# One transformer-like layer in fp32: the rotary step moved from GpSimd to VectorE, and three changes to the order of the output products

## The chip, the core and the metric

The kernel runs on one core of a Trainium2 chip. The metric is the device time of one execution in microseconds (us), shown as the median of three runs. The core has five engines that each follow their own list of instructions: TensorE (PE, with its weight loads as PEld), VectorE (DVE), ScalarE (ACT), GpSimd (POOL) and SyncE (SP), which issues most of the transfers (DMA). They wait for each other through semaphores; each executes its list in order.

## What is computed

One layer over 2,048 prompt tokens and 32 sample tokens, model width 1,024, everything in fp32. Cut to what matters here:

```python
h = rmsnorm(x, ln_g)
q, k, v, gate_a, b_gate, c_gate, u_in, gate_c, merge_a, merge_c = split(h @ w_in)
q = rope(rmsnorm(q.reshape(b, t, 8, 64), q_norm_g), pos)     # per head of 64
k = rope(rmsnorm(k.reshape(b, t, 2, 64), k_norm_g), pos)
attn = banded attention of q, k, v in chunks of 64, with sinks
y_a = (attn * silu(gate_a)) @ w_attn_out                     # "yA", 512 -> 1024
y_c = (b_gate * conv3(c_gate * u_in) * silu(gate_c)) @ w_conv_out   # "yB"
r = x + (sigmoid(merge_a) * y_a + sigmoid(merge_c) * y_c) @ w_o     # "o"
out = r + sigmoid(r @ w_ple_gate) * (p @ w_ple_proj)         # "pg" and "pp"
```

The rotary step of one head x with halves x1, x2 is `[x1*cos - x2*sin, x2*cos + x1*sin]`. Since the norm's factor is one number for a head and token, it may be applied ahead of the rotation or behind it.

## The kernel before

**Products.** Every operand of a matmul is split into a high and a low part (`hi` by an ACT cast, `lo` by a DVE subtraction), and each product is three matmuls. So each piece of weights, 128x512 numbers, costs an ACT cast and a DVE subtraction after its load. All of this keeps PE at 98% of the span.

**Two stages.** The first stage (to 855 us of the span) makes h @ w_in and writes q, k, v, the gates and the conv rows to DRAM. The change touches only the second stage, which starts there: attention in 17 tiles of 128 tokens (one of 32), woven by single matmuls into the output products. Tokens stand in four blocks b of 512 (the last has 544). A unit of products is named by kind, block and column group: `yB0_3`, `pp2_1`, `yA0_4`, `o0_2`, `pg0_7`. Blocks 1 and 2 share Strassen-like products for o and pg (`b50_n_p` and `b58_n_p`: matrix 50 is w_o, 58 is w_ple_gate, p one of seven products, n a column group), and block 3 makes them by quadrants (`s50..`, `s58..`).

**What sets the order.** `plan` (line 272) lists the units by hand. While the program is written, a planner in the kernel keeps a clock `now` with fixed prices for each engine and writes instructions in the order of that clock; helpers are generators that hand back their needs (`yield {"ps": 2}` asks for two PSUM banks) and go on when these are free. So most instructions of the second stage have the line of the recording helper, L135, and are told apart by tiles. Nothing is reordered at run time: an instruction that waits holds up those behind it on its engine.

**The rotary step** (`attention`, from line 1310). For a tile, PE transposes q and k, v into PSUM (`pq`, `pkv`). ACT squares them into `qn`, DVE sums the squares (`ss`), adds EPS, and GpSimd takes the power -1/2 and makes `ab`, cos and sin times the norm weights. DVE then multiplies q and k from PSUM by `ss` into `qn` (128x512 and 128x128). The rest is GpSimd's: the products `tt` with cos and sin (128x256 for k, 128x1024 for q), and the sums `kr` (two of 128x128) and `qr` (two of 128x256). PE transposes `kr` and `qr` (`pk`, `pqt`), ACT and DVE split them (`KH`/`KL`, `qs`), and the scores `S` follow. GpSimd also issues the transfers that add a DRAM row to a row in SBUF (`ta<-z_t`, `tk<-z_t`, `c<-in_xT`).

**Other names that are used below.** `ta`, `tk`: rows of yA with their gate; `m_l`, `ac_l`, `p_l`, `xb_l`, `r_l`, `rq_l`: low parts of rows for the next product; `pf`: rows of p as loaded; `w<-wr`: the split of a weight piece; `at<-O,ga`: a chunk's output times its gate; `nm<-S`, `se`: the softmax's maximum and sum; `ptl`, `pth`: the transposed probabilities.

**Weights and rows.** `next_loads` issues a raw piece when one of 8 raw buffers is free and it is under 8 pieces beyond the split ones (five); `split_w` splits pieces in order. `load_p` loads rows of p; block 3's are loaded again for each pair of `pp` units (four times).

## Time and profile before

| | us |
|---|---|
| median of 3 runs | 1529.82 |
| lowest, highest run | 1529.79, 1532.02 |
| the profiled execution | 1532.24 |
| its span, first to last instruction | 1530.5 |
| PE busy | 1501.7 (98%) |
| DVE busy | 1206.2 (79%) |
| ACT busy | 836.3 (55%) |
| POOL busy | 468.3 (31%) |
| the second stage, from yB's first product to the last matmul's end | 855.8 to 1525.5 |

A row of the trace gives the start (us from the span's start), the duration, engine, line, operation, `out<-in` by tiles, and in brackets how long the engine was idle ahead of it and who ended that. A matmul's bar is longer than the time to the next one, since matmuls overlap; so waits are read from PE's idle brackets and from the difference of a window's length and PE's busy time.

### The profile page before, as it was taken

How to read it: one execution, taken by the hardware profiler on the slowest of the kernel's cores; microseconds unless marked ns; L12 is line 12 of the kernel's file. 1: busy time of each engine (PE TensorE's matmuls, PEld its weight loads, DVE VectorE, ACT ScalarE, POOL GpSimd, SP SyncE). 2: the span in 40 equal slices, each digit the busy share in tenths (PEclk: the TensorE clock that was granted, in tenths of full speed). 3: DMA queues.
4: the chain of work that ended last, by engine and by line, in shares of the span. 5: the costliest groups of instructions: out<-in, count | busy, mean ns of one | idle time of the engine just before them, and what ended most of it. 6: DMA issues, size and time to landing. Idle time of an engine off the chain costs nothing.

```text
span 1530.5 us, 27077 instructions
## 1 busy us (share of the span) xinstructions
PE 1501.7 (98%) x9025; PEld 1333.8 (87%) x9025; DVE 1206.2 (79%) x2208; ACT 836.3 (55%) x1966; POOL 468.3 (31%) x634
## 2 busy tenths in 40 slices
PE   9999999999999999999999999989999999999898
PEld 7878888888889999999999889978887877888898
DVE  7896887875589766898955787898967789785886
ACT  8453354344467544434554566767775475653575
POOL 2133332332212232333232245462433334112112
PEclk9999999999999999999999999999999999999999
DMA  9479886798778845343555786685678838879998
GB/s 341 154 280 342 308 293 232 276 342 279 241 266 268 307 141 196 117 132 115 184 191 185 266 302 216 217 245 188 201 193 217 220 93 205 223 209 319 289 311 253
DMA packets 207292, 357.94 MB, mean 234 GB/s; under 512 B 24624, under 2 KB 61552, under 8 KB 207152
## 3 DMA queue, kind: packets, MB, share of 16 engines
q1 hardware_dynamic: 165216, 252.40, 50.9%
q0 software_dynamic: 32288, 85.99, 19.3%
q10 hardware_dynamic: 9648, 17.83, 3.1%
q8 instruction: 71, 1.16, 0.3%
q14 instruction: 69, 0.57, 0.1%
HBM read 238.77 MB, written 117.46 MB: 233 GB/s over the span
## 4 chain that ended last, share of the span: by engine, by line
PE 41%; DVE 5%; DMA 4%; issue 2%; ACT 1%; SPq 0%; POOL 0%; DVEq 0%; ACTq 0%
PE b L135 7%; PE yB L135 6%; PE yA L135 3%; PE o L135 3%; PE pg L135 3%; PE O L135 2%; DMA pf<-in_pT 2%; PE S L135 2%; PE s58a L135 1%; PE la L722 1%; DMA wr<-in_wu 1%; PE a L589 1%; PE a L586 1%; PE a L584 1%; PE s50a L135 1%
## 5 line engine op out<-in xcount | busy, mean ns | idle before, releaser
L586 PE MATMUL a<-x_l,w 128*128 128x264 f32 (+1 forms) x744 | 228.2, 319 | 0.0
L584 PE MATMUL a<-x_h,w 128*128 128x264 f32 (+1 forms) x744 | 227.3, 320 | 0.4 <-DVE s L790 0.4
L589 PE MATMUL a<-x_h,w 128*128 128x264 f32 (+1 forms) x744 | 201.4, 320 | 0.0
L135 ACT CAST w<-wr 128x512 fp32r<-128x512 f32 x204 | 123.7, 621 | 87.2 <-PE b L135 30.9
L135 DVE TENSOR_TENSOR w<-wr,w 128x512 fp32r<-128x512 f32 x204 | 154.0, 765 | 18.3 <-ACT w L135 16.8
L206 ACT CAST w<-wr 128x512 fp32r<-128x512 f32 (+1 forms) x180 | 110.1, 618 | 105.8 <-PE c L589 30.7
L207 DVE TENSOR_TENSOR w<-wr,w 128x512 fp32r<-128x512 f32 (+1 forms) x180 | 131.0, 738 | 36.9 <-ACT w L206 35.6
L584 PEld LDWEIGHTS a<-x_h,w 128*128 128x128 f32 x744 | 139.8, 188 | 11.0 <-DVE s L790 0.6
L586 PEld LDWEIGHTS a<-x_l,w 128*128 128x128 f32 x744 | 140.1, 188 | 10.3
L135 PE MATMUL b<-xb_h,w 128*128 128x512 f32 x448 | 142.7, 395 | 1.8 <-ACT w L135 1.1
L589 PEld LDWEIGHTS a<-x_h,w 128*128 128x128 f32 x744 | 125.2, 188 | 10.8
L722 PE MATMUL la<-x_h,w 128*128 128x264 f32 x516 | 111.9, 285 | 1.7 <-ACT w L206 1.2
L584 PE MATMUL c<-x_h,w 128*128 128x512 f32 (+1 forms) x336 | 110.5, 339 | 0.0
L586 PE MATMUL c<-x_l,w 128*128 128x512 f32 (+1 forms) x336 | 110.4, 338 | 0.0
L135 PEld LDWEIGHTS b<-xb_h,w 128*128 128x128 f32 x448 | 83.4, 188 | 21.0 <-DVE w L135 1.6
L206 ACT CAST w<-a 128x512 fp32r<-128x512 f32 x82 | 49.7, 620 | 94.3 <-DVE a L342 30.9
L589 PE MATMUL c<-x_h,w 128*128 128x512 f32 (+1 forms) x336 | 99.9, 338 | 0.0
L783 DVE SCALAR_TENSOR_TENSOR u<-u,c 128x264 f32<-128x264 f32 (+1 forms) x125 | 59.4, 507 | 42.7 <-ACT u L778 28.4
L778 ACT COPY u<-a 128x264 f32<-128x264 f32 (+1 forms) x114 | 47.4, 437 | 79.7 <-PE a L589 75.5
L135 PE MATMUL yA<-ac_h,w 128*128 128x512 f32 (+1 forms) x320 | 89.0, 358 | 1.6 <-DVE ta L135 1.0
L722 PEld LDWEIGHTS la<-x_h,w 128*128 128x128 f32 x516 | 87.0, 189 | 2.4 <-ACT w L206 1.4
L135 PE MATMUL b<-xb_l,w 128*128 128x512 f32 x224 | 88.3, 394 | 0.0
(535 smaller groups left out, 4310.2 us busy)
## 6 DMA issues: line engine op xcount, KB each, us to landing
wr<-in_wu SPq DMA_DIRECT2D x213, 256.0 KB, 4.2
a<-in_wu SPq DMA_DIRECT2D x116, 256.0 KB, 5.1
wr<-ws SPq DMA_DIRECT2D x74, 256.0 KB, 3.5
wr<-qs SPq DMA_DIRECT2D x64, 256.0 KB, 4.6
ws<-a POOLq DMA_DIRECT2D x63, 256.0 KB, 3.8
qs<-a POOLq DMA_DIRECT2D x24, 256.0 KB, 5.7
tb<-z_t SPq DMA_DIRECT2D x24, 256.0 KB, 4.9
z_t<-tb SPq DMA_DIRECT2D x24, 256.0 KB, 4.3
```

The costliest lines, as they stand in the source:

```text
L135: return f(**kw)
L206: nc.scalar.copy(out=hi, in_=src)
L207: nc.vector.tensor_tensor(out=lo, in0=src, in1=hi.bitcast(F32), op=sub)
L584: nc.tensor.matmul(out=ps[:, :cn], lhsT=w[:, 0, k], rhs=x[0][:, c0:c0 + cn], start=first and k == 0, stop=False, skip_group_check=True)
L586: nc.tensor.matmul(out=ps[:, :cn], lhsT=w[:, 0, k], rhs=x[1][:, c0:c0 + cn], start=False, stop=False, skip_group_check=True)
L589: nc.tensor.matmul(out=ps[:, :cn], lhsT=w[:, 1, k], rhs=x[0][:, c0:c0 + cn], start=False, stop=k == 3, skip_group_check=True)
L722: nc.tensor.matmul(out=ps[:, :m], lhsT=w[:, a, k], rhs=r[:, cols], start=q in "ABG" and j == 0 and e == 0, stop=j == 1 and e == 2, skip_gr ...
L778: nc.scalar.copy(out=t[:, c0:c0 + cn], in_=ps[:, :cn])
L783: nc.vector.scalar_tensor_tensor(out=t[:, c0:c0 + cn], in0=t[:, c0:c0 + cn], scalar=-1.0, in1=ps[:, :cn], op0=mul, op1=sub)
```

## The change

Five edits, all in the second stage.

1. The rotary step. `ab` is made first, on GpSimd. DVE multiplies q and k straight from PSUM with `ab` into `tt`, without the norm's factor; ACT squares into a tile `sq` whose 65th column holds EPS, so that the sum includes it; DVE adds the halves into `kn` and `qr`; and at the end DVE multiplies by `ss` into `kr` and `qr`. GpSimd keeps the power and `ab`.
2. `plan`'s start: yB of blocks 0 and 1 first, then yB of 2 and 3 with pp of block 2 between; pp of block 3, units 2 to 5, among and behind yA of block 0 instead of near the end.
3. `plan`'s end: block 3's yA stands among pg's products from the 18th of 28 on (before: from the 22nd, with the last one behind all), and two pg products come behind the last yA.
4. Weights: raw pieces are loaded up to eleven ahead of the piece in use, and a split buffer is given back 0.5 us (of the planner's clock) after its last use.
5. Rows of p for block 3: three loads instead of four.

```diff
-    plan = [("yB", b + e, n) for b in (0, 2) for n in range(8) for e in range(2)]
-    plan += [("pp", 2, n) for n in range(8)] + [("yA", 0, n) for n in range(8)] + [("pp", 3, 0), ("pp", 3, 1)]
+    plan = [("yB", e, n) for n in range(8) for e in range(2)]
+    for n in range(8):
+        plan += [("yB", 2, n), ("yB", 3, n), ("pp", 2, n)]
+    plan += [("pp", 3, 0), ("pp", 3, 1)] + [("yA", 0, n) for n in range(5)]
+    plan += [("pp", 3, 2), ("yA", 0, 5), ("pp", 3, 3), ("yA", 0, 6), ("yA", 0, 7), ("pp", 3, 4), ("pp", 3, 5)]
...
-    plan += tail[:21]
-    for e, part in enumerate(tail[21:]):
-        plan += [part, ("yA", 3, NA[3][e])]
-    plan += [("pp", 3, 2), ("pp", 3, 3), ("yA", 3, NA[3][7]), ("pp", 3, 4), ("pp", 3, 5)]
+    plan += tail[:17]
+    late = [("yA", 3, n) for n in NA[3]]
+    for e, part in enumerate(tail[17:27]):
+        plan += [part] + ([late.pop(0)] if e not in (2, 9) else [])
+    plan.append(tail[27])
...
+        ab = sm.tile([P, 2, 2, 64], F32, tag="ab", name=f"ab{b}_{i}", bufs=1)
+        eG.tensor_tensor(out=ab[:n], in0=cs[:n].unsqueeze(1).to_broadcast([n, 2, 2, 64]),
+                        in1=qkg_sb[:n].unsqueeze(2).to_broadcast([n, 2, 2, 64]), op=mul)
...
+        for q, (h0, hn, src) in enumerate(q3):
+            eV.tensor_tensor(out=tt[:n, h0:h0 + hn], in0=src[:n].unsqueeze(2).to_broadcast([n, hn, 2, 64]),
+                            in1=ab[:n, q].unsqueeze(1).to_broadcast([n, hn, 2, 64]), op=mul)
...
-        eV.tensor_reduce(out=ss[:n], in_=qn[:n], axis=AX.X, op=add)
-        eV.tensor_scalar(out=ss[:n], in0=ss[:n], scalar1=EPS, scalar2=None, op0=add)
+        eV.tensor_reduce(out=ss[:n], in_=sq[:n], axis=AX.X, op=add)
...
+        for d in (0, 32):
+            for o, h in ((kn, slice(8, 10)), (qr, slice(0, 8))):
+                eV.tensor_tensor(out=o[:n, :, d:d + 32], in0=tt[:n, h, 0, d:d + 32], in1=tt[:n, h, 1, 32 - d:64 - d], op=add)
...
-        for h0, hn, src in q3[::-1]:
-            eV.tensor_tensor(out=qn[:n, h0:h0 + hn], in0=src[:n], op=mul,
-                            in1=ss[:n, h0:h0 + hn].unsqueeze(2).to_broadcast([n, hn, 64]))
...
-        for h0, hn, q in ((8, 2, 1), (0, 8, 0)):
-            eG.tensor_tensor(out=tt[:n, h0:h0 + hn],
...
-        for d in (0, 32):
-            eG.tensor_tensor(out=qr[:n, :, d:d + 32], in0=tt[:n, 0:8, 0, d:d + 32],
-                            in1=tt[:n, 0:8, 1, 32 - d:64 - d], op=add)
+        eV.tensor_tensor(out=kr[:n], in0=kn[:n].unsqueeze(2).to_broadcast([n, 2, 2, 64]),
+                        in1=ss[:n, 8:10].unsqueeze(2).unsqueeze(3).to_broadcast([n, 2, 2, 64]), op=mul)
+        eV.tensor_tensor(out=qr[:n], in0=qr[:n], in1=ss[:n, 0:8].unsqueeze(2).to_broadcast([n, 8, 64]), op=mul)
...
-        while n_raw[0] < len(worder) and busy["Y"] < now[0] + 0.5 and (
-                n_raw[0] < RAWS or raw_free[n_raw[0] - RAWS] <= now[0]) and n_raw[0] < len(made) + RAWS:
+        while n_load[0] < min(len(worder), used[0] + LOOK) and busy["Y"] < now[0] + 0.5:
...
-    for i, at_ in enumerate(("yB2_5", "yA0_2", f"yA3_{NA[3][2]}", f"yA3_{NA[3][4]}", f"s{UO}_2_2")):
+    for i, at_ in enumerate(("yB0_7", "yB2_5", "yA0_3", f"s{UO}_2_2")):
```

How the rows of an engine move is seen best at two places. The first is the tile `2_0` (the first of block 2), whose rotary step stands among the last yA of block 0. GpSimd's list there before, from the tile's power to the end of its sums:

```order
L135 TENSOR_TENSOR ss2_0_12274<-ss2_0_12274,nhalf_70 128x10
L135 TENSOR_TENSOR ab2_0_12316<-cs2_0_12091,cst_69 128x256
L135 DMA ta0_4_12121<-z_t1_4_112 128x512
L135 TENSOR_TENSOR tt2_0_12383<-qn2_0_12261,ab2_0_12316 128x256
L135 DMA ta0_5_12166<-z_t1_5_113 128x512
L135 TENSOR_TENSOR tt2_0_12383<-qn2_0_12261,ab2_0_12316 128x1024
L135 TENSOR_TENSOR kr2_0_12385<-tt2_0_12383 128x4x32 x2
L135 TENSOR_TENSOR qr2_0_12384<-tt2_0_12383 128x8x32 x2
```

and in the changed kernel:

```order
L135 DMA ta0_3_12143<-z_t1_3_111 128x512
L135 DMA ta0_4_12170<-z_t1_4_112 128x512
L135 TENSOR_TENSOR ab2_0_12403<-cs2_0_12183,cst_69 128x256
L135 TENSOR_TENSOR ss2_0_12453<-ss2_0_12453,nhalf_70 128x10
L135 DMA ta0_5_12284<-z_t1_5_113 128x512
L135 COPY KH_10068<-KH_10068 128x2x128
```

The six products and sums are gone from GpSimd. On DVE before, the same tile has the two multiplications by `ss` and, behind them, what DVE does while GpSimd works on the tile:

```order
L135 TENSOR_TENSOR qn2_0_12261<-pkv2_0_12253,ss2_0_12274 128x128
L135 TENSOR_TENSOR qn2_0_12261<-pq2_0_12248,ss2_0_12274 128x512
L135 SCALAR_TENSOR_TENSOR ta0_5_12166<-ta0_5_12166,yA0_5_0_12285 128x512
L135 TENSOR_TENSOR KL_10069<-pk1_3_12328,KH_10068 128x2x128
L135 SCALAR_TENSOR_TENSOR ta0_6_12222<-ta0_6_12222,yA0_6_0_12347 128x512
L135 TENSOR_TENSOR qs1_3_12342<-pqt1_3_12331,qs1_3_12342 64x2x256
L135 SCALAR_TENSOR_TENSOR m0_3_l_12367<-ta0_3_12069,m0_3_h_12366 128x512
L135 TENSOR_TENSOR ta0_6_12222<-ta0_6_12222,tc0_6_12224 128x512
L135 TENSOR_TENSOR qs1_3_12342<-pqt1_3_12331,qs1_3_12342 64x2x256
```

and in the changed kernel, the tile's end:

```order
L135 TENSOR_TENSOR kn2_0_12415<-tt2_0_12413 128x2x32
L135 TENSOR_TENSOR qr2_0_12414<-tt2_0_12413 128x8x32
L135 TENSOR_TENSOR kn2_0_12415<-tt2_0_12413 128x2x32
L135 TENSOR_TENSOR qr2_0_12414<-tt2_0_12413 128x8x32
L135 SCALAR_TENSOR_TENSOR ta0_6_12367<-ta0_6_12367,yA0_6_0_12505 128x512
L135 RECIPROCAL se_14_12526<-se_14_12526 128x4
L135 TENSOR_TENSOR w390_12547<-wr390_12145,w390_12547 128x512
L135 TENSOR_TENSOR at1_2_12112<-O_12_12554,ga1_2_12110 128x4x64
L135 TENSOR_TENSOR kr2_0_12416<-kn2_0_12415,ss2_0_12453 128x256
L135 TENSOR_TENSOR qr2_0_12414<-qr2_0_12414,ss2_0_12453 128x512
```

DVE now holds four sums and two scalings of the tile in its own list, and two products from PSUM ahead of them. The second place is ACT's list near the end, where block 3's yA and the last pg products are made. Before, the rows of p (`p2`, `p3`) are split there, among the weight pieces:

```order
L135 ACTIVATE rq1_50_0_h_16659<-ta3_4_16455 128x544
L135 CAST p2_0_h_16676<-pf2_0_16586 128x544
L135 ACTIVATE c21_58_0_6_16089<-c21_58_0_6_16089 128x512
L135 CAST p2_1_h_16684<-pf2_1_16597 128x544
L135 ACTIVATE rq2_50_0_h_16661<-rta50_0_16669 128x544
L135 ACTIVATE rq3_50_0_h_16663<-rtb50_0_16670 128x544
L135 CAST w487_16728<-wr487_16450 128x512
L135 CAST w488_16741<-wr488_16484 128x512
```

and in the changed kernel the same rows of block 3's first `rq` tiles:

```order
L135 ACTIVATE rq1_50_0_h_16625<-ta3_4_16443 128x544
L135 CAST w484_16651<-wr484_16415 128x512
L135 ACTIVATE rq2_50_0_h_16627<-rta50_0_16636 128x544
L135 CAST w485_16675<-wr485_16452 128x512
L135 ACTIVATE rq3_50_0_h_16629<-rtb50_0_16637 128x544
L135 ACTIVATE c11_58_1_1_15992<-c11_58_1_1_15992 128x512
```

The splits of p are no longer in this part of ACT's list.

## The prediction

> **What bounds the kernel now.** I read the engines' busy shares first: PE is busy for 1501.7 of 1530.5 us, so the change can only win what PE waits, some 28 us with both ends of the program. The second stage alone is touched, so I took it in windows of 50 us and looked for those where PE's busy time falls short of 50. These are the four that lose most, and one that loses nothing (busy us of each engine, granted clock, DMA share):

> ```profile
> core 0: us, PE busy (x) PEld busy (x) DVE busy (x) ACT busy (x) POOL busy (x), PEclk, DMA share, GB/s
> 1000.00:1050.00 50.00, 44.21 (x243) 38.17 (x242) 45.78 (x71) 33.46 (x97) 21.40 (x22) 0.97 0.74 208
> 1050.00:1100.00 50.00, 50.00 (x284) 43.04 (x284) 45.04 (x85) 38.07 (x115) 22.25 (x20) 1.00 0.64 202
> 1150.00:1200.00 50.00, 47.13 (x242) 38.92 (x241) 37.36 (x62) 27.89 (x86) 18.15 (x19) 0.97 0.90 238
> 1250.00:1300.00 50.00, 47.26 (x234) 39.13 (x233) 47.40 (x75) 29.14 (x73) 24.70 (x26) 1.00 0.74 178
> 1400.00:1450.00 50.00, 44.59 (x299) 41.22 (x298) 42.31 (x82) 26.05 (x53) 7.84 (x9) 0.97 0.98 297
> ```

> PE waits there 5.79 + 2.87 + 2.74 + 5.41 = 16.81 us. In three of them the granted clock is 0.97, which costs 0.03 × 50 = 1.5 us each, 4.5 together. So 21.3 us are to be had. PE's waits in the second stage, longest total first, name whom it waited for:

> ```profile
> PE S L135 <- DVE qs L135: 5.5, 2, 3.8
> PE yA L135 <- DVE ac_l L135: 2.9, 1, 2.9
> PE s50b L135 <- DVE w L135: 1.8, 1, 1.8
> PE pqt L135 <- DVE at L135: 1.8, 1, 1.8
> ```

> Nearly all end with DVE. Why is DVE late, at 79% busy? The longest wait, of 3.80 us, shows it in three timelines, of PE, DVE and GpSimd (start, duration, in brackets the idle time ahead):

> ```profile
> 1033.83 0.33 PE L135 MATMUL S<-KH,qs 128*128 128x192 f32 x1 [3.80 <-DVE qs L135]
> ```

> ```profile
> 1019.26 0.80 DVE L135 TENSOR_REDUCE ss<-qn 128x10 f32<-128x640 f32 x1
> 1020.10 0.17 DVE L135 TENSOR_SCALAR ss<-ss 128x10 f32<-128x10 f32 x1
> ...
> 1022.55 1.03 DVE L135 TENSOR_REDUCE nm<-S 128x2 f32<-128x386 f32 x2
> 1023.50 0.68 DVE L135 SCALAR_TENSOR_TENSOR m_l<-ta,m_h 128x512 fp32r<-128x512 f32 x1
> 1024.09 0.28 DVE L135 TENSOR_TENSOR qn<-pkv,ss 128x128 f32<-128x128 f32 x1
> 1024.29 0.68 DVE L135 TENSOR_TENSOR qn<-pq,ss 128x512 f32<-128x512 f32 x1
> 1024.89 0.68 DVE L135 SCALAR_TENSOR_TENSOR ta<-ta,yA 128x512 f32<-128x512 f32 x1
> 1025.49 0.42 DVE L135 TENSOR_TENSOR KL<-pk,KH 128x256 fp32r<-128x256 f32 x1
> 1025.82 0.68 DVE L135 SCALAR_TENSOR_TENSOR ta<-ta,yA 128x512 f32<-128x512 f32 x1
> 1026.53 0.68 DVE L135 TENSOR_TENSOR qs<-pqt,qs 64x512 fp32r<-64x512 f32 x1
> 1027.24 4.92 DVE L135 SCALAR_TENSOR_TENSOR m_l<-ta,m_h 128x512 fp32r<-128x512 f32 x1
> 1032.09 0.88 DVE L135 TENSOR_TENSOR ta<-ta,tc 128x512 f32<-128x512 f32 x1
> 1032.99 0.69 DVE L135 TENSOR_TENSOR qs<-pqt,qs 64x512 fp32r<-64x512 f32 x1
> ```

> ```profile
> 1026.69 2.70 POOL L135 TENSOR_TENSOR tt<-qn,ab 128x1024 f32<-128x1024 f32 x1
> 1029.06 1.15 POOL L135 TENSOR_TENSOR kr<-tt 128x128 f32<-128x128 f32 x2
> 1029.89 1.65 POOL L135 TENSOR_TENSOR qr<-tt 128x256 f32<-128x256 f32 x2
> ```

> The same `m_l` takes 0.68 us at 1023.50 and 4.92 us at 1027.24, where it lies beside GpSimd's `tt`, `kr` and `qr` from start to end. Steps of DVE that read PSUM (`qs` at 1026.53) keep their 0.68 us beside `tt`; those with all operands in SBUF don't. In the groups of the second stage this stands as means above 680 ns:

> ```profile
> L135 DVE TENSOR_TENSOR w<-wr,w 128x512 fp32r<-128x512 f32 x188 | 143.4, 771 | 16.8 <-ACT w L135 15.4 <-DMA wr<-in_wu 0.5
> ...
> L135 DVE SCALAR_TENSOR_TENSOR ac_l<-acf,ac_h 128x512 fp32r<-128x512 f32 x12 | 12.3, 1039 | 0.3 <-ACT ac_h L135 0.2
> ...
> L135 DVE SCALAR_TENSOR_TENSOR m_l<-ta,m_h 128x512 fp32r<-128x512 f32 x8 | 9.6, 1212 | 0.0
> ...
> L135 DVE TENSOR_TENSOR tk<-tk,tk 128x512 f32<-128x512 f32 x4 | 6.6, 1640 | 0.0
> ```

> That is 188 × 0.091 + 12 × 0.359 + 8 × 0.532 + 4 × 0.960 = 17.1 + 4.3 + 4.3 + 3.8 = 29.5 us of DVE over the 680 ns.

> **The rotary step.** Prices of DVE's steps from start to start are 0.20 us for 128 numbers wide (1024.09 to 1024.29), 0.33 for 256 (1025.49 to 1025.82) and 0.60 for 512 (1024.29 to 1024.89): about 1.04 ns a number and 0.07 fixed. Removed for a tile: 0.20 + 0.60 for the two multiplications by `ss`, 0.08 for EPS (at most its 0.17), so 0.88. Added: `tt` of q, 1024 wide, 0.07 + 1.06 = 1.13 by the slope; it reads PSUM with a repeated operand, which no row shows, so its ends are 0.60 (as if 512) and GpSimd's 2.70; I take the slope, since both DVE sizes from PSUM lie on it. `tt` of k 0.33; `kn` 2 × 0.13; `qr` 2 × 0.33; the scaled `kr` 0.33 and `qr` 0.60. Sum 3.31, net 2.43, and for 16 full tiles 39 us. Against it go the 29.5 us of those four groups, and the like in smaller ones. DVE's sum stays about equal; what changes is that no step takes 4.92 us at a bad moment, and that the chain of a tile no longer passes over GpSimd for some 4.85 us (1026.69 to the end of `qr`, 1031.54).

> In the changed order `tt` on DVE waits for ACT's square of the same bank, and ACT's copy of v waits for `tt`. The square takes

> ```profile
> L135 ACT ACTIVATE qn<-pq 128x512 f32<-128x512 f32 x16 | 9.5, 596 | 11.5 <-PE pq L135 9.2 <-DMA z_t<-u 2.0
> ```

> so DVE loses between 0 and 0.60 us a tile, at most 10 us over 17 tiles. Queued behind it on DVE are weight splits and `ta` sums; no matmul of that tile is. I take nothing for PE. [...]

> Where DVE's new load is tightest is between the products of tile `1_2` and those of `2_1`. The changed order has there on DVE 52 steps of 512, 27 of 256, 18 of 64, 12 `nm`, 6 reciprocals, 3 `tt` of q, 3 `ss`, and three others: 52 × 0.60 + 27 × 0.33 + 18 × 0.13 + 12 × 0.47 (1022.55 to 1023.50, two) + 6 × 0.09 + 3 × 1.13 + 3 × 0.73 + 1.6 = 56 us, with estimates for the small ones and for `ss` (0.80 at 1019.26 less the overlap). PE's products there, by rows of the chain of waits (start, length, count),

> ```profile
> 1042.65 0.87 PE S L135 x8
> ...
> 1264.89 16.14 PE b L135 x70
> ...
> 1468.63 3.00 PE s50a L135 x24
> ```

> come to 121 × 0.231 + 74 × 0.125 + some 174 small × 0.11 = 56.3 us. So DVE is 99% full for these 56 us: the 5.79 us of the first window will not all go. Their ends are 0 and, if DVE's steps stay at the 771 ns of `w` (13% over 680), 56 × 0.13 − 0.3 = 7 us. I take 3.0. For 1150 and 1250 I leave 1.0 each of 2.87 and 2.74: the cause (`ac_l`, `w`, `tk` at twice their time, and `qr` on GpSimd ahead of the `pqt` wait) goes, but DVE is at 47.40 of 50 in the second, and the first has a DMA share of 0.90.

> The clock follows the waits. It is 0.83 in the 10 us behind the wait of 2.87 us, which ends at 1169.52:

> ```profile
> 1160.00:1170.00 10.00, 7.13 (x39) 5.75 (x38) 9.28 (x15) 7.84 (x28) 6.69 (x5) 1.00 1.05 332
> 1170.00:1180.00 10.00, 10.00 (x49) 7.77 (x47) 7.59 (x13) 4.99 (x12) 4.55 (x6) 0.83 0.57 111
> ```

> If the long waits go, the 4.5 us go with them. [...]

> **The ends of the plan.** Near 1400 the rows of p come late for ACT, and weights and `ta` queue behind them:

> ```profile
> 1409.15 0.65 ACT L135 CAST p_h<-pf 128x544 fp32r<-128x544 f32 x1 [2.90 <-DMA pf<-in_pT]
> ...
> 1420.68 1.32 ACT L135 CAST p_h<-pf 128x544 fp32r<-128x544 f32 x2 [4.30 <-DMA pf<-in_pT]
> ```

> at a DMA share of 0.98. The change takes these four casts, their two loads, two weight pieces, the four `pp` units' stores and DVE's four low parts out of this stretch. They land among the last yA of block 0, where the DMA share is 0.64 to 0.74; one pair of rows goes altogether. In exchange the last yA has two pg products behind it instead of two pp units. Twelve matmuls of 0.231 make 2.77 us, so the cover is 5.5 us against the units' 2 × 1.5 = 3.0 (24 rows of 0.125 are 3.00): no cost, and up to 2 us if the final sums fall behind the last product. Of 5.41 I leave 1.5, since the share stays high.

> **Weights ahead.** Eleven raw or split pieces feed 11 × 2.77 = 30 us, and a load lands in 4.2:

> ```profile
> wr<-in_wu SPq DMA_DIRECT2D x213, 256.0 KB, 4.2
> ```

> So the shorter reach costs nothing. Were the cover gone, the price is that of the `s50b` wait on `w`, 1.8 us each time; a gain has no row either.

> **The sum.** 21.3 − (3.0 + 1.0 + 1.0 + 1.5) = 14.8 us. The profiled execution took 1532.24 us, its span and 1.7 around it, and would come to 1517.4; it was 2.4 above the median. From the median of 1529.82: 1515.0. A measurement tells about 0.2%, 3.1 us, from no change, so "same" is 1526.8 to 1532.9.

> **The rivals.** *Everything goes and nothing comes* (0.15): the slow DVE steps were the only cause; 1529.8 − 21.3 = 1508.5. For it: 1050 to 1100 holds 50.00 with DVE at 45.04. Against it: the 99%.

> *DVE becomes the bound* (0.14): its steps keep the 13%. Then the 56 us lose 7; block 3's tiles, 35.4 us of DVE for 37.0 of PE by the same count, lose 40.0 − 37.0 = 3.0; the clock's 4.5 stay; of 1150 and 1400 another 4 stay. 21.3 − 18.5 = 2.8 us: 1527. For it: 45.78 and 47.40 of 50 in the waiting windows. Against it: the cause of the 13% is gone from GpSimd, but for `ab` and the power.

> *The tile's chain is late on DVE: slower* (0.11). GpSimd did its sums beside DVE; now they stand in DVE's list, and a tile's `pk` and `pqt` wait for all that is queued ahead of `kr` and `qr`. Behind the products of tile `1_2` PE has 8.8 us of other work up to `pk`, and DVE 8.4 us of rows. Two more rows of 0.60 ahead of the scaling, and the ping-pong's 0.60, make 9.6 + 0.6 − 8.8 = 1.4 us of wait. The point from which it decides is 21.3 / 17 = 1.3 us a tile. At 1.6 us each it costs 27 and gives 1535.5. Against it: the other tiles have about 14 us of PE there.

> *The order does not do what it says* can't be for the rotary step, as the order shows GpSimd without it. That the slow DVE steps have another cause lies within the second rival.

> **How the numbers follow.** My forecast has 0.60, with 1509 to 1522 for its own range: the 6.5 us left in can be 0.5 to 13.5. With 0.15 for 1508.5 and 0.14 around 1527, a third of it under 1526.8, faster has 0.60 + 0.15 + 0.05 = 0.80; same takes the rest of that rival, 0.09; slower 0.11. The range runs from 1506, a little under the clean case, to 1527.

> **What would show it.** Right: in the changed profile no `w`, `m_l`, `ac_l` or `tk` far above 680 ns; `tt` on DVE near 1.2 us; PE's 3.80 and 2.87 us waits gone, with the granted clock at 1.00 behind them; no p rows between 1400 and 1435; what waits are left stand between tiles `1_2` and `2_1`, and end with DVE. Wrong: `pk` or `pqt` waiting for DVE's `kr` or `qr` in most tiles; the 13% still there; `tt` nearer to 2.7 us; or waits for weights that the eleven don't cover.

## The result, and the profile after

The changed kernel takes 1523.13 us (median of 5 runs, 1520.78 to 1524.68), beside 1529.82 for the kernel before (5 runs, 1528.82 to 1532.02). The ratio is 0.9947, with a 95% interval of 0.9936 to 0.9959: 6.7 us faster, where 14.8 were forecast. The profiled execution took 1523.18 us, with a span of 1521.4.

The windows of the second stage that the prediction spoke of, and the one ahead of them, in the changed kernel (busy us of each engine, then clock, DMA share and GB/s):

```profile
core 0: us, PE busy (x) PEld busy (x) DVE busy (x) ACT busy (x) POOL busy (x), PEclk, DMA share, GB/s
...
950.00:1000.00 50.00, 48.02 (x333) 43.94 (x331) 41.74 (x99) 36.81 (x121) 7.83 (x8) 0.99 0.73 228
1000.00:1050.00 50.00, 48.54 (x271) 41.04 (x271) 42.73 (x88) 37.27 (x118) 13.48 (x12) 0.90 0.79 224
...
1150.00:1200.00 50.00, 49.91 (x268) 41.86 (x267) 34.69 (x68) 30.39 (x90) 12.87 (x14) 1.00 0.93 253
...
1250.00:1300.00 50.00, 50.00 (x241) 41.16 (x240) 45.14 (x84) 30.87 (x80) 13.79 (x14) 1.00 0.74 188
...
1400.00:1450.00 50.00, 45.38 (x299) 42.36 (x298) 37.56 (x71) 24.44 (x47) 8.71 (x10) 0.93 0.94 265
```

Put into one table, a window's loss is what PE's busy time lacks of 50 us, and behind the plus what the clock lacks of 1.00, times 50:

| window | before | left by the forecast | changed kernel |
|---|---|---|---|
| 950 to 1000 | 0 | 0 | 1.98 + 0.5 |
| 1000 to 1050 | 5.79 + 1.5 | 3.0 | 1.46 + 5.0 |
| 1150 to 1200 | 2.87 + 1.5 | 1.0 | 0.09 |
| 1250 to 1300 | 2.74 | 1.0 | 0 |
| 1400 to 1450 | 5.41 + 1.5 | 1.5 | 4.62 + 3.5 |
| sum | 21.3 | 6.5 | 17.2 |

So the places behind 1100 went as forecast or better, and the first yA (around 1000) and the last yA (around 1420) did not. The windows give 4.1 us; the profiled executions differ by 9.1. The windows' clock term is too large where PE also stood idle at half clock, since idle time loses nothing by it: in the changed kernel PE was idle for 3.1 of the 17.1 us at half clock.

A closer account goes by the distances from the start of one matmul to the next. Each product has a usual distance at full clock (its median over the traces). The 3,790 matmul records of the second stage add up to 640.7 us by it, in every kernel here. What a distance has beyond it is waiting, and where the clock was half, the doubling of the usual distance is put down to the clock. The doubling is the author's estimate: back to back, products of yA stand 0.43 us apart at half clock and 0.23 at full, those of `s50a` 0.23 and 0.13 (the traces of before and after). By this the stage took 669.4 us before, with 23.2 of waiting and 5.5 of clock, and takes 660.6 in the changed kernel, with 13.9 of waiting and 6.1 of clock. So the gain is 9.4 us of waiting, and the clock gave nothing.

PE's longest waits are others than before:

```profile
PE s50a L135 <- DVE w L135: 2.5, 1, 2.5
PE yA L135 <- ACT ac_h L135: 1.8, 2, 1.3
PE s50b L135 <- DVE w L135: 1.4, 1, 1.4
...
PE pk L135 <- DVE kr L135: 0.4, 1, 0.4
```

The wait of 3.80 us for `qs` and that of 2.87 us for `ac_l` are gone. Around the first yA the waits are small, but windows of 5 us show what lies behind them:

```profile
995.00:1000.00 5.00, 3.02 (x20) 2.10 (x18) 5.00 (x14) 4.33 (x13) 0.00 (x0) 0.94 0.94 282
1000.00:1005.00 5.00, 4.14 (x7) 1.58 (x6) 3.23 (x6) 3.57 (x11) 0.00 (x0) 0.50 0.49 189
1005.00:1010.00 5.00, 4.75 (x22) 4.47 (x22) 1.32 (x5) 2.61 (x8) 0.00 (x0) 0.53 0.06 17
```

TensorE runs at half its clock for 10 us. What PE waits for ahead of that and in it stands in its timeline (idle time and releaser in brackets), and the engine behind it is ACT, which waits for rows:

```profile
996.81 0.41 PE L135 MATMUL pk<-cst,kr 128*128 128x128 f32 x2 [0.44 <-DVE kr L135]
997.41 0.63 PE L135 MATMUL pqt<-cst,qr 128*128 128x128 f32 x4 [0.19 <-ACT S L135]
999.39 0.79 PE L135 MATMUL yA<-ac_h,w 128*128 128x512 f32 x1 [1.35 <-ACT ac_h L135]
...
1002.06 0.80 PE L135 MATMUL yA<-ac_h,w 128*128 128x512 f32 x1 [0.46 <-ACT ac_h L135]
```

```profile
1001.38 0.63 ACT L135 ACTIVATE ac_h<-acf 128x512 fp32r<-128x512 f32 x1 [2.05 <-DMA acf<-z_at]
```

`acf` holds block 0's attention rows, which are stored to DRAM (`z_at`) when the block's last tile ends and are loaded again. SP's list in the changed kernel has these transfers at

```profile
986.99 0.56 SPq L135 DMA_DIRECT2D z_at<-at  x1
...
993.62 0.38 SPq L135 DMA_DIRECT2D acf<-z_at  x1
```

and in the kernel before at

```profile
980.70 0.56 SPq L135 DMA_DIRECT2D z_at<-at  x1
...
985.18 0.87 SPq L135 DMA_DIRECT2D acf<-z_at  x2
```

Tile `0_3`'s rows come 6.3 us later and their load starts 8.4 us later, while the first yA stands only 3 us later (996.5 before, 999.4 now).

DVE's groups can be held against the prices of the prediction (count, busy us, mean ns, idle ahead of them):

```profile
L135 DVE TENSOR_TENSOR w<-wr,w 128x512 fp32r<-128x512 f32 x188 | 129.2, 694 | 19.8 <-ACT w L135 17.0 <-PE b L135 1.5
...
L135 DVE TENSOR_TENSOR tt<-pq,ab 128x1024 f32<-128x1024 f32 x16 | 19.5, 1220 | 6.1 <-ACT sq L135 6.1
...
L135 DVE SCALAR_TENSOR_TENSOR ac_l<-acf,ac_h 128x512 fp32r<-128x512 f32 x12 | 7.9, 682 | 1.7 <-ACT ac_h L135 1.7
...
L135 DVE SCALAR_TENSOR_TENSOR m_l<-ta,m_h 128x512 fp32r<-128x512 f32 x8 | 5.5, 686 | 0.5 <-ACT m_h L135 0.3
```

The slow steps are gone: `m_l` went from 1212 to 686 ns, `w` from 771 to 694.

### The profile page after: what moved, and what is told of

The parts are those of the page before. It is cut to its first block, busy times and chain, and to the rows that moved or that the text cites. A ratio compares the mean times of both kernels' runs of the same rounds, so it can differ in the third digit from the quotient of the medians.

```text
span 1521.4 us, 27059 instructions
## 1 busy us (share of the span) xinstructions
PE 1501.7 (99%) x9025; PEld 1334.0 (88%) x9025; DVE 1205.0 (79%) x2291; ACT 835.1 (55%) x1964; POOL 370.3 (24%) x533
## 5 line engine op out<-in xcount | busy, mean ns | idle before, releaser
L135 ACT CAST w<-wr 128x512 fp32r<-128x512 f32 x204 | 124.6, 620 | 75.5 <-PE yA L135 17.7
L135 DVE TENSOR_TENSOR w<-wr,w 128x512 fp32r<-128x512 f32 x204 | 139.7, 693 | 21.4 <-ACT w L135 18.5
L135 PE MATMUL b<-xb_h,w 128*128 128x512 f32 x448 | 142.0, 394 | 0.0
L135 PEld LDWEIGHTS b<-xb_h,w 128*128 128x128 f32 x448 | 83.6, 188 | 17.9
L796 DVE SCALAR_TENSOR_TENSOR u<-u,c 128x264 f32<-128x264 f32 (+1 forms) x125 | 59.4, 506 | 43.8 <-ACT u L791 27.3
L135 PE MATMUL yA<-ac_h,w 128*128 128x512 f32 (+1 forms) x320 | 90.4, 360 | 2.3 <-ACT ac_h L135 1.8
L135 PE MATMUL b<-xb_l,w 128*128 128x512 f32 x224 | 88.5, 395 | 0.0
## 6 DMA issues: line engine op xcount, KB each, us to landing
wr<-in_wu SPq DMA_DIRECT2D x213, 256.0 KB, 4.1
a<-in_wu SPq DMA_DIRECT2D x116, 256.0 KB, 5.1
wr<-ws SPq DMA_DIRECT2D x74, 256.0 KB, 3.4
wr<-qs SPq DMA_DIRECT2D x64, 256.0 KB, 4.8
ws<-a POOLq DMA_DIRECT2D x63, 256.0 KB, 4.0
qs<-a POOLq DMA_DIRECT2D x24, 256.0 KB, 5.8
tb<-z_t SPq DMA_DIRECT2D x24, 256.0 KB, 4.4
z_t<-tb SPq DMA_DIRECT2D x24, 256.0 KB, 4.0
```

Of the source, the lines that this page charges most:

```text
L135: return f(**kw)
L796: nc.vector.scalar_tensor_tensor(out=t[:, c0:c0 + cn], in0=t[:, c0:c0 + cn], scalar=-1.0, in1=ps[:, :cn], op0=mul, op1=sub)
```

## The experiments

Theory after the result: GpSimd's SBUF work did slow DVE, and the new rotary step pays that back by making the tiles of block 0 end later. Rival: the gain is the order's alone. The planner lays out the whole second stage anew for each edit of the order, so an edit also shifts things elsewhere, and 2 or 3 us between two kernels need not come from the place that was edited.

**Rotary step and order apart.** The first kernel is the one before with the rotary edits alone.

```diff
 # kernel before
-            eG.tensor_tensor(out=tt[:n, h0:h0 + hn],
...
+            eV.tensor_tensor(out=tt[:n, h0:h0 + hn], in0=src[:n].unsqueeze(2).to_broadcast([n, hn, 2, 64]),
...
+        eV.tensor_tensor(out=qr[:n], in0=qr[:n], in1=ss[:n, 0:8].unsqueeze(2).to_broadcast([n, 8, 64]), op=mul)
```

> The kernel before with the rotary step of the change alone: old order, old rule for weights, old loads of p. Theory (GpSimd's SBUF work slowed DVE, and the changed order is what brings the loss at the first yA): the waits at 1000, 1150 and 1250 go with 3.0 us of clock, the old loss at 1400 to 1450 (5.41 us and 1.5 of clock) stays, and the eight pp units still stand ahead of the first yA, so no wait there: 1529.8 - 11.4 - 3.0 = 1515, at most 1519. Rival (the order and the weights bring the gain, the rotary step moves cost from GpSimd to DVE and is worth nothing): 1528 to 1532.

Measured: 1534.27 us, beside 1530.63 for the kernel before in the same series; ratio 1.0021 (1.0012 to 1.0031). The rotary step alone makes the kernel slower. DVE's `w` is at 694 ns here too, and the wait of 3.80 us for `qs` is gone; instead `O` waits 3.6 us in all for `ptl` and 1.2 for `pth`, and yA 4.2 for the rows `ac`, most of it between 989 and 1005.

```profile
950.00:1000.00 50.00, 44.87 (x287) 40.69 (x286) 40.46 (x95) 37.64 (x123) 8.65 (x8) 0.93 0.67 213
1000.00:1050.00 50.00, 47.59 (x258) 39.81 (x258) 42.63 (x87) 37.63 (x111) 11.84 (x12) 0.93 0.72 196
...
1150.00:1200.00 50.00, 48.40 (x254) 40.65 (x253) 32.49 (x64) 28.35 (x80) 11.69 (x13) 1.00 0.89 236
1200.00:1250.00 50.00, 49.71 (x253) 41.50 (x252) 40.65 (x81) 28.61 (x78) 10.93 (x10) 1.00 0.54 142
1250.00:1300.00 50.00, 50.00 (x250) 41.44 (x250) 46.51 (x87) 33.27 (x84) 14.38 (x18) 1.00 0.77 191
```

From 1150 to 1300 this kernel loses 1.9 us, where the kernel before lost 6.1 and 1.5 of clock, so there the step does what was forecast. From 950 to 1050 it loses 7.5 + 7.0, where the kernel before lost 5.8 + 1.5. The theory's reason holds in its first half, its forecast does not: the late first yA belongs to the step itself, also in the old order.

The other half is the changed kernel with the old rotary step.

```diff
 # changed kernel
-            eV.tensor_tensor(out=tt[:n, h0:h0 + hn], in0=src[:n].unsqueeze(2).to_broadcast([n, hn, 2, 64]),
...
+            eG.tensor_tensor(out=tt[:n, h0:h0 + hn],
...
```

> The changed kernel with the old rotary step on GpSimd: new order, new weights, new loads of p alone. Theory: DVE's w stays at 771 ns and the waits beside GpSimd stay, elsewhere: 1526 to 1531. Rival (the order brings the gain): 1521 to 1524.

Measured: 1519.27 us; ratio 0.9925 (0.9909 to 0.9942). The rival is right on this, and by more than it said: order and weights give 11.4 us by themselves, and with the rotary step 6.7. Its group of `w` and its waits before 1400:

```profile
L135 DVE TENSOR_TENSOR w<-wr,w 128x512 fp32r<-128x512 f32 x188 | 152.2, 819 | 22.2 <-ACT w L135 21.5
```

```profile
PE O L135 <- DVE ptl L135: 2.0, 2, 1.8
PE pq L135 <- DMA zq<-z_q: 0.6, 1, 0.6
```

`w` is slower than in the kernel before (819 against 771 ns), with GpSimd's sums still there, and yet PE's longest wait before 1400 is 1.8 us. So the slow DVE steps are real, but what PE waits for depends on which product stands behind them.

**GpSimd's traffic put back.** To test the slowing itself, the changed kernel gets work on GpSimd that nobody needs, without a change in the order of PE or DVE.

```diff
 # changed kernel
         eG.tensor_tensor(out=ss[:n], in0=ss[:n], in1=nhalf[:n, 0:10], op=ALU.pow)
         pow_done = fin[0]
+        for _ in range(3):
+            nc.gpsimd.tensor_tensor(out=sq[:n, :, 0:64], in0=sq[:n, :, 0:64], in1=sq[:n, :, 0:64], op=add)
```

> The changed kernel with three additions of 128x640 in SBUF on GpSimd for each tile, behind the power, that nothing needs; the order on PE and DVE is the same, and the output stays the reference's. Theory (GpSimd's SBUF work slows DVE's steps whose operands are all in SBUF): the mean of w goes from 693 ns to over 750, waits of PE that end with DVE come back, 1529 to 1536. Rival (DVE's slow steps came from elsewhere, or cost PE nothing): 1522 to 1525.

Measured: 1536.23 us; ratio 1.0032 (1.0021 to 1.0043), by the ratios 13 us over the changed kernel.

```profile
L135 DVE TENSOR_TENSOR w<-wr,w 128x512 fp32r<-128x512 f32 x188 | 140.0, 753 | 17.6 <-ACT w L135 14.1 <-PE b L135 1.5 <-DMA out_yT<-tg 0.8
```

```profile
PE pk L135 <- DVE kr L135: 4.6, 2, 2.7
```

`w` went to 753 ns, and `pk` waits for `kr`. In this trace no wait of PE, ACT or DVE in the second stage ends with GpSimd, so the ballast did not hold them up by a semaphore. From 855 to 1400 DVE is busy for 467.9 us here, for 442.4 in the changed kernel, 436.8 with the old step in the new order and 434.6 before. So the ballast shows the slowing: added on top of the new step it costs 13 us. Taken away in exchange for DVE's own steps, 39 us by the prediction's estimate, it leaves DVE's total where it was.

**Cover ahead of the first yA.** Four pp units of block 3 stand ahead of yA instead of two.

```diff
 # changed kernel
-    plan += [("pp", 3, 0), ("pp", 3, 1)] + [("yA", 0, n) for n in range(5)]
-    plan += [("pp", 3, 2), ("yA", 0, 5), ("pp", 3, 3), ("yA", 0, 6), ("yA", 0, 7), ("pp", 3, 4), ("pp", 3, 5)]
+    plan += [("pp", 3, n) for n in range(4)] + [("yA", 0, n) for n in range(8)] + [("pp", 3, 4), ("pp", 3, 5)]
```

> The changed kernel with two more pp units of block 3 (3.0 us of PE) ahead of the first yA. Theory (the rows ac for the first yA land too late, 3.4 us of waits near 997 to 1005 and 5.1 us at half clock behind them): most of both goes, 1523.1 - 7 = 1516. Rival (the waits there come from DVE's and ACT's load at the tile, not from the rows): they move with the tile, 1522 to 1524.

Measured: 1519.56 us; ratio 0.9923 (0.9906 to 0.9940). PE's waits there:

```profile
1000.01 0.49 PE L135 MATMUL yA<-ac_h,w 128*128 128x512 f32 x1 [0.30 <-ACT ac_h L135]
1000.74 0.50 PE L135 MATMUL yA<-ac_l,w 128*128 128x512 f32 x1 [0.23 <-DVE ac_l L135]
1003.15 0.50 PE L135 MATMUL yA<-ac_h,w 128*128 128x512 f32 x1 [0.60 <-ACT ac_h L135]
```

The tile ends as late as in the changed kernel (its last `at` at 986.4 and 986.5 us), but 3.0 us more products stand ahead; the waits shrink and the half clock is gone (1.00 in both windows from 950 to 1050). That shows the late rows as the cause there. From 950 to 1050 the loss falls from 8.9 to 3.1 us, clock included; 1.9 of what is left are two waits of pp units for DVE near 1035. The whole kernel got half of the expected 7 us.

The same edit with the old rotary step, which has no such wait:

```diff
 # changed kernel with the old rotary step
-    plan += [("pp", 3, 0), ("pp", 3, 1)] + [("yA", 0, n) for n in range(5)]
...
+    plan += [("pp", 3, n) for n in range(4)] + [("yA", 0, n) for n in range(8)] + [("pp", 3, 4), ("pp", 3, 5)]
```

> The new order and weights with the old rotary step, and two more pp units of block 3 ahead of the first yA. Theory (the new rotary step loses because its tiles end later and the rows ac of the first yA land late; the old one has no wait there, so there is nothing to cover): 1518 to 1521, so that both rotary steps give the same once the rows are covered (1519.6 with the new one). Rival (the two pp units are worth 3.6 us wherever they stand, and the rotary step costs its 3.9 us by its load on DVE): 1515 to 1516.5.

Measured: 1523.24 us; ratio 0.9938 (0.9926 to 0.9951): nothing is gained, as the theory says, and 2 us or so may be lost, more than it said. The edit is worth something only with the new rotary step. With it, 0.9923 and the changed order with the old step, 0.9925, can't be told apart: once its late rows are covered, the new step costs nothing that these runs show, and brings nothing either.

**The order taken apart**, all with the old rotary step: the rule for weights alone, the plan's start alone, and both without the new end.

```diff
 # kernel before: weights alone
-        while n_raw[0] < len(worder) and busy["Y"] < now[0] + 0.5 and (
...
+        while n_load[0] < min(len(worder), used[0] + LOOK) and busy["Y"] < now[0] + 0.5:
```

> The kernel before with the new rule for weights alone (eleven pieces ahead, split buffers given back later); old order, old rotary step. Theory (the start of the plan brings the gain of the order, since four pp units, which cost DVE nothing, stand where DVE is fullest): 1528 to 1531. Rival (the weights bring it): 1519 to 1523.

Measured: 1529.01 us beside 1531.27 in that series; ratio 0.9987 (0.9979 to 0.9996): about 2 us.

```diff
 # kernel before: start alone
+    plan = [("yB", e, n) for n in range(8) for e in range(2)]
...
-    plan += [("pp", 3, 2), ("pp", 3, 3), ("yA", 3, NA[3][7]), ("pp", 3, 4), ("pp", 3, 5)]
+    plan += [("yA", 3, NA[3][7])]
```

> The kernel before with the new start of the plan alone (yB, pp and the four pp units of block 3 among yA of block 0, three loads of p), block 3's yA at their old places with the last one behind all of pg's products; old weights, old rotary step. Theory (the start brings the gain): 1519 to 1524, and the waits at 1027 to 1034 and at 1169 are gone with their clock. Rival (the weights bring it): 1527 to 1531.

Measured: 1533.04 us; ratio 1.0009 (1.0000 to 1.0017). Neither alone is the gain. Its window at the end shows why the start doesn't pay by itself:

```profile
1400.00:1450.00 50.00, 43.85 (x270) 40.17 (x269) 38.04 (x76) 22.04 (x41) 7.85 (x9) 0.86 0.91 267
```

It loses 6.15 + 7.0 us there, where the kernel before lost 6.9 in all: the pp units that stood behind the last yA are gone, and nothing took their place. The third kernel has start and weights, but the old end:

```diff
 # changed kernel with the old rotary step
-    plan += tail[:17]
...
+    plan += tail[:21]
+    for e, part in enumerate(tail[21:]):
+        plan += [part, ("yA", 3, NA[3][e])]
+    plan += [("yA", 3, NA[3][7])]
```

> The new order and weights with the old rotary step, and with block 3's yA back at their old places, the last one ahead of the quadrants with no pg product behind it. Theory (the rows ta and the weights are late there on a full DMA either way): within 2 us of 1519.3. Rival (the two pg products behind the last yA cover 5.5 us of waits, as was predicted): 1523 to 1525.

Measured: 1525.87 us; ratio 0.9962 (0.9948 to 0.9976), and the same window:

```profile
1400.00:1450.00 50.00, 41.71 (x261) 38.95 (x261) 39.41 (x78) 24.52 (x47) 9.14 (x11) 0.86 0.87 255
```

8.29 + 7.0 us are lost there. With the new end (0.9925) it is 4.67 + 3.5, so the new end repays what moving the pp units uncovered, and the rival is right as far as that. The edit takes back the new places of yA and the two pg products behind the last one together, so it doesn't show which of the two it was. Against the kernel before, the stretch gains nothing. Start and weights together bring 5.8 us (0.9962), where alone they bring 2.0 and cost 1.4; why they help each other isn't settled.

**The last yA.** In the changed kernel, DVE, ACT and PE near 1420:

```profile
1418.69 0.44 DVE L135 SCALAR_TENSOR_TENSOR ta<-ta,yA 128x272 f32<-128x272 f32 x1 [3.57 <-DMA ta<-z_t]
...
1422.51 0.69 DVE L135 TENSOR_TENSOR w<-wr,w 128x512 fp32r<-128x512 f32 x1
```

```profile
1419.87 0.66 ACT L135 ACTIVATE rq_h<-rta 128x544 fp32r<-128x544 f32 x1 [3.02 <-DVE rta L135]
1420.43 0.60 ACT L135 CAST w<-wr 128x512 fp32r<-128x512 f32 x1
```

```profile
1423.25 0.59 PE L135 MATMUL s50a<-rq_h,w 128*128 128x272 f32 x1 [2.54 <-DVE w L135]
```

The row `ta` is issued two units ahead and lands 7 to 11 us later. DVE's list waits 3.57 us for it, and ACT's list for what DVE makes of it. From 1418.69 on DVE works without a pause through the steps that were queued behind the row, and only then, at 1422.51, splits the weight piece that PE waits for. Two edits give the row more time: yA spread wider, or rows loaded three units ahead.

```diff
 # changed kernel with two more pp units ahead of yA, and the new order with the old rotary step
-    plan += tail[:17]
...
+    plan += tail[:14]
...
+    for e, part in enumerate(tail[14:27]):
+        plan += [part] + ([late.pop(0)] if e not in (2, 4, 6, 8, 10) else [])
```

> The changed kernel with two more pp units ahead of the first yA, and block 3's yA spread from the 15th pg product on instead of the 18th. Theory (what is left near 1420 is the rows ta of the last yA, which land 7 to 11 us after their issue while ACT's list, with the weights in it, waits for them): more pg products between the yA give the rows time, 1519.6 - 4 = 1515 to 1517. Rival (the DMA engines are full there, share 0.93 and more, so whatever stands there is late): 1518 to 1521.

Measured: 1520.45 us; ratio 0.9939 (0.9925 to 0.9953).

> The new order and weights with the old rotary step, and block 3's yA spread from the 15th pg product on. Theory as for the run before it: 1519.3 - 4 = 1515 to 1517. Rival (DMA full): 1518 to 1521.

Measured: 1521.25 us; ratio 0.9945 (0.9933 to 0.9957). With the new rotary step the stretch stays at 45.30 of 50; with the old one it rises to 47.56 with the clock at 0.97, but `pq` now waits 4.4 us for its rows near 1185. The theory's place is right in one of two, its total in neither.

```diff
 # new order with the old rotary step; and the changed kernel with two more pp units ahead of yA
-    LEAD, AHEAD_S, LOOK = 2, 5, 11
+    LEAD, AHEAD_S, LOOK = 3, 6, 11
```

> The new order and weights with the old rotary step, and the rows of a unit (ta, tb, pp) loaded three units ahead instead of two. Theory (the rows ta are issued too late for their 7 to 11 us): the waits at 1419 go, 1515 to 1517. Rival (the DMA engines are full there, or the row buffers run out): 1518 to 1523.

Measured: 1516.11 us beside 1530.20; ratio 0.9910 (0.9897 to 0.9923), the fastest kernel of all. It is clear of the changed one, but not of the same order without the edit (0.9925, to 0.9909 at the low end). The edit also loads the rows of block 3's quadrant products six units ahead instead of five.

```profile
1400.00:1450.00 50.00, 47.03 (x321) 44.36 (x320) 40.23 (x77) 27.45 (x54) 8.67 (x10) 0.97 0.98 293
```

The loss there falls from 4.67 + 3.5 to 2.97 + 1.5 us at a DMA share of 0.98, so a full DMA wasn't all of the limit: the row was asked for too late.

> The changed kernel with two more pp units ahead of the first yA and the rows of a unit loaded three units ahead. Theory: 1519.6 - 4 = 1515 to 1517. Rival (DMA full, or the row buffers run out): 1518 to 1523.

Measured: 1520.51 us; ratio 0.9937 (0.9924 to 0.9950). The stretch gains as much (47.09, clock 0.97), but 1.2 us are lost between 875 and 900, and 2.66 between 1150 and 1200, where `pq` waits 1.0 us for its rows. The place answers to the theory, the total to the rival. So loading earlier is shown to help at 1420 in both kernels, and the whole kernel is not shown to be faster by it in either.

## Why the prediction was right in direction and too large

**The prices of the step held.** `tt` of q was put at 1.13 us from start to start, and is 1.22 as a bar, less the 0.08 of overlap 1.14. DVE waits 6.1 us for ACT's squares, inside the 0 to 10 given; PE's wait for `kr` is 0.4 us in all. "DVE's sum stays about equal" held too (434.6 and 442.4 us). In the changed order DVE and ACT wait for each other, `tt` those 6.1 us for the squares and ACT's copies of v 15.7 us for `tt`; no wait of PE in this trace ends with either.

**What failed first is the step from slow instructions to PE's waits.** The sum let the loss at 1000, 1150 and 1250 go because GpSimd's work on the tile goes, and gave the plan's start and the weights nothing. The account of the second stage by the distances between matmuls, one profiled execution of each kernel, in us (the one with the rotary step alone is the fastest of its 12 runs):

| kernel | second stage | waiting | clock |
|---|---|---|---|
| before | 669.4 | 23.2 | 5.5 |
| rotary step alone | 671.4 | 23.2 | 7.5 |
| order and weights alone | 657.3 | 13.6 | 3.0 |
| both, the changed kernel | 660.6 | 13.9 | 6.1 |
| both, four pp units ahead of the first yA | 657.3 | 13.9 | 2.8 |

DVE's slow steps went with the rotary step, and PE waited as long as before in all: what was won from 1150 to 1300 came back at the first yA. The order and the weights took 9.7 us of waiting away although `w` stood at 819 ns. Either half alone takes the wait of 3.80 us for `qs` away; that of 2.87 for `ac_l` is down to 1.60 with the rotary step alone and gone with the order alone. The rotary step costs 0.21% alone. In the new order the account gives it 3.3 us, 3.0 of them clock; the ratios with and without it (0.9947 and 0.9925) say much the same, though their intervals just overlap. So the time came out inside 1506 to 1527 in part by luck: the forecast's own 1509 to 1522 was missed by 1 us, and the gain has another source than the one that was given.

**The term around 1000 had its size by luck.** The 3.0 us were for a full DVE between the products of tiles `1_2` and `2_1`. In the changed kernel that stretch runs from 988.2 to 1057.3; DVE was busy for 59.4 us of it, near the 56 of the estimate, and PE's busy time falls short by 3.4 us. But 3.1 of these stand at the first yA (1.98 + 0.86 + 0.25 in the three windows of 5 us above). By PE's brackets 2.4 us there end with `ac_h` or `ac_l`, the splits of tile `0_3`'s late rows, which were in no term and brought some 5 us of clock with them; 0.44 us end with DVE's `kr`, at the end of a rotary step. The last 0.35 us, at 1035.7, end with ACT. So a full DVE, the cause that was given, has at most 0.44 us of it directly.

The prediction looked at the step's chain inside a tile, which did get shorter: 10 to 15 us now from `pq` to `pk` in the four tiles from `0_3` on, 17 to 21 before. It did not look at when the next tile may start: these four tiles start at 927.1, 945.5, 966.1 and 986.6 us, and before at 918.8, 934.3, 951.0 and 979.0. Now `pq` comes behind the tile ahead's `pk` (939.6 and 945.5), where before it came ahead of it (934.3 and 939.1). Whether the buffers of the new step or DVE's list set this wasn't tried on the chip, and why the tiles start later stays open.

**The clock.** "If the long waits go, the 4.5 us go with them" failed: the clock was half for 10.24 us and for 6.83 us, behind waits of at most 2.54 us, where before it was half three times for 3.41 us. Short waits were enough; the last section has them added up.

**The end.** "Of 5.41 I leave 1.5" failed: 4.62 and more clock. The rows of p were out of the way, and the row `ta` was late next; the prediction named `ta` as queued behind p, not as late itself. That the new end is needed was right: without it, the spread of yA and the cover of two pg products together, the stretch loses 8.29 + 7.0.

**Weights.** "The shorter reach costs nothing" is not the whole of it: the rule alone gains some 2 us (0.9979 to 0.9996), for which the prediction had no row.

Of the rivals, none came as such. The saturated DVE (1527) has the right kind of sum, most of the gain given back, by another mechanism; the late tile chain decided at the first yA alone, not in each tile.

## What to carry to other kernels

What DVE's slowed steps cost PE here depended on the product that stood behind them (with `w` at 819 ns PE's longest wait before 1400 was 1.8 us, with `w` at 771 it was 3.80), so ask of each long wait whether an edit of the order would take it away more cheaply than an edit of the work. When a step moves, follow not only its own chain but the start of the next tile and the rows that the last tile leaves for the next phase. When late transfers are moved out of a stretch, look for the next late row in the same list and ask whether it was issued too late. Add up waiting and clock over the whole stage too: a wait that goes in one window can come back in another.

## What the runs showed of the hardware

**GpSimd and DVE on SBUF.** Three additions of 128x640 on GpSimd for each tile raised the mean of DVE's `w`, whose operands are all in SBUF, from 694 to 753 ns, while two steps on DVE that read one operand from PSUM stayed the same: `tt`, which in its own tile ends ahead of the additions (1220 and 1222 ns), and `qs` (689 and 688).
